# Splitting the load of x by partitions instead of by columns in an 8-expert MLP: staging, semaphores and the last wait

## The chip, the cores and the metric

The kernel runs on one core of a Trainium2 chip. The metric is the device time of one execution in microseconds (us); lower is better. The core has a matrix engine (PE), a vector engine (DVE), a scalar engine (ACT), a general engine (Pool, GpSimd) and a sync engine (SP), each with its own program, and 16 DMA engines that move data between the DRAM (HBM) and the on-chip memory SBUF. SBUF has 128 partitions, and a tensor in it is written [partitions, elements of each partition]. PSUM is the small memory that PE writes its sums to.

## The reference

Eight experts, each with its own weights; no routing, every expert has its 256 rows.

```python
n_experts, capacity, hidden, expert_hidden = 8, 256, 512, 2048
# x [8, 256, 512], w1 [8, 512, 2048], w2 [8, 2048, 512], all float32
h = np.matmul(x, w1)
h = np.maximum(h, 0)
return np.matmul(h, w2).astype(np.float32)
```

The weights are 67.1 MB of float32, x is 4.19 MB and the output 4.19 MB.

## The kernel before

**Layout.** Weights and x are cast to bf16 on the way in. `w1_sb` and `w2_sb` have four slots each (`NS = 4`); expert e uses slot e mod 4. x is first put, rows as they are, into slot 2 of `w2_sb`, under the name `x_sb`: [128, 8192] bf16, where partition p holds 16 rows of x. In DRAM, a partition's 16 rows are 32 KB without a gap. PE transposes it from there into `xT`. `hT` holds the hidden activations of one expert and `out_sb` [128, 8, 2, 512] float32 all outputs. The tensors have fixed places from byte `FIRST_FREE` on; below that, 8 KB were left for the staging tile `x_head`.

**Loading x.** x comes in two parts. The head, the first four of each partition's 16 rows, is loaded by SP as float32 into `x_head` and cast by DVE into `x_sb` (lines 116 and 117). The other twelve rows of each partition are loaded by Pool with the cast done by the DMA (line 131). DMAs issued by Pool are called software_dynamic in the profile, those of SP hardware_dynamic.

**Order of the weights.** All weight loads are issued by Pool, in the order of the list `loads` (lines 99 to 105): w1 and w2 of experts 0 and 1 together, then of 2 and 3, then w1 of 4 and 5, and from there single experts; the last w2 is cut into two halves. A load into a slot that was used before waits until PE has done the expert that used it. The w2 load of experts 2 and 3 overwrites `x_sb`, so it waits for the transposes. Just ahead of the very last weight load stands a tiny store of a few outputs (line 160), which later tells Pool by `d_pool` that the queue has got that far; then Pool stores the outputs of experts 0 to 6 in one transfer (line 172). SP waits for each load in turn and passes it on to PE (`c_w1`, `c_w2`, lines 121 to 123), and at the end stores the outputs of the last expert (line 125).

**Compute.** PE makes the transposes (lines 278 to 304), and then runs a loop over experts: two `half` passes fill `h_ps`, ACT applies the ReLU into `hT` (line 213), and 32 matmuls make `o_ps`, which DVE copies to `out_sb` (line 196); for the last expert ACT copies one half (line 219). The matmul instructions all come from a helper and have line 252, and PE's waits have line 227.

**Semaphores.** PE announces its events on three: `p_xt` (transposes), `p_h` (groups of hidden values) and `p_o` (outputs). `s_ident` counts the two steps that make the identity matrix, `v_out` two points at which DVE has finished outputs. At the very end:

```python
pool.drain()
act.wait_ge(d_pool, 48)
act.wait_ge(d_last, 16).then_inc(s_ident)
```

`d_pool` reaches 48 when the big store has landed, `d_last` 16 when the last one has. After this comes a closing barrier of all engines.

## Time and profile before

| | |
|---|---|
| time, median of 3 | 180.68 us (180.66 to 180.76) |
| span, first to last instruction | 178.9 us |
| PE busy | 129.4 us (72%) |
| ACT, DVE, Pool busy | 38.7, 15.8, 10.3 us |
| moved by DMA | 40.37 MB, mean 226 GB/s |
| Pool's DMA queue, share of 16 engines | 97.2% |
| head of x: size, issue to landing | 1024 KB, 4.9 us |
| rest of x: size written, issue to landing | 1536 KB, 11.6 us |
| weight loads: issue to landing | 43 to 51 us |

The DMA figures count bytes written. A load that turns float32 into bf16 writes half of what it reads, so the same reading rate shows as half the GB/s. "Issue to landing" includes the time that a transfer stands in line behind those issued before it. Where the profile names `w_sb`, it means `w1_sb` or `w2_sb`. "PEq" and "SPq" are the instruction sequencers of those engines.

### The profile page before, as it was taken

How to read it: one execution, taken by the hardware profiler on the slowest of the kernel's cores; microseconds unless marked ns; L12 is line 12 of the kernel's file. 1: busy time of each engine (PE TensorE's matmuls, PEld its weight loads, DVE VectorE, ACT ScalarE, POOL GpSimd, SP SyncE). 2: the span in 40 equal slices, each digit the busy share in tenths (PEclk: the TensorE clock that was granted, in tenths of full speed). 3: DMA queues.
4: the chain of work that ended last, by engine and by line, in shares of the span. 5: the costliest groups of instructions: out<-in, count | busy, mean ns of one | idle time of the engine just before them, and what ended most of it. 6: DMA issues, size and time to landing. Idle time of an engine off the chain costs nothing. (4 is left out here: it accounts for less than half of the span.)

```text
span 178.9 us, 2103 instructions
## 1 busy us (share of the span) xinstructions
PE 129.4 (72%) x832; PEld 90.5 (51%) x832; DVE 15.8 (9%) x20; ACT 38.7 (22%) x38; POOL 10.3 (6%) x21
## 2 busy tenths in 40 slices
PE   0008610793049999995079999999999999969990
PEld 0007610692013696594024884794695696359630
DVE  0204320000000200110000200200200200110010
ACT  0202420053000044044000251152062044004400
POOL 6100010000000002001000100100010000002000
PEclk9999999999756999999859999999999999987997
DMA  6999998999999999899899999999989999999995
GB/s 211 244 216 209 234 227 183 234 231 194 220 234 201 209 234 223 187 234 231 187 227 234 201 209 234 216 194 234 227 187 231 231 194 220 234 189 219 334 423 243
DMA packets 3744, 40.37 MB, mean 226 GB/s; under 512 B 288, under 2 KB 288, under 8 KB 1312
## 3 DMA queue, kind: packets, MB, share of 16 engines
q0 software_dynamic: 3456, 38.80, 97.2%
q1 hardware_dynamic: 288, 1.57, 2.4%
HBM read 71.30 MB, written 4.20 MB: 422 GB/s over the span
## 5 line engine op out<-in xcount | busy, mean ns | idle before, releaser
L252 PE MATMUL o_ps<-w_sb,hT 128*128 x256 | 61.3, 401 | 17.8 <-PEq L227 17.8
L252 PE MATMUL h_ps<-xT,w_sb 128*128 x512 | 62.2, 284 | 11.3 <-PEq L227 11.3
L252 PEld LDWEIGHTS h_ps<-xT,w_sb 128*128 x512 | 58.4, 146 | 15.9 <-issue 13.1
L213 ACT ACTIVATE hT<-h_ps 128x1024 bf16<-128x1024 f32 x32 | 32.7, 1023 | 111.2 <-PE h_ps L252 111.2
L252 PEld LDWEIGHTS o_ps<-w_sb,hT 128*128 128x128 bf16 x256 | 25.6, 102 | 50.7 <-issue 24.5
L196 DVE COPY out_sb<-o_ps 128x512 f32<-128x512 f32 x15 | 9.7, 686 | 141.2 <-PE o_ps L252 141.2
L252 PE MATMUL xt_ps<-identity,w_sb 128*128 128x128 bf16 x64 | 7.6, 311 | 15.6 <-PEq L227 15.6
L252 PEld LDWEIGHTS xt_ps<-identity,w_sb 128*128 x64 | 6.5, 146 | 16.4 <-issue 16.4
L169 POOL DMA_DIRECT2D w_sb<-in_w_dram x12 | 7.4, 619 | 105.1 <-PE h_ps L252 58.0
L179 ACT COPY xT<-xt_ps 128x1024 bf16<-128x1024 bf16 x4 | 4.0, 1012 | 11.7 <-PE xt_ps L252 11.7
L179 DVE COPY xT<-xt_ps 128x1024 bf16<-128x1024 bf16 x4 | 4.9, 1224 | 11.9 <-PE xt_ps L252 11.9
L172 POOL DMA_DIRECT2D out_dram<-out_sb x1 | 1.0, 966 | 33.3 <-DMA out_dram<-out_sb 33.3
L179 ACT ACT_TABLE_LOAD x1 | 1.3, 1283 | 7.2 <-DVE w_sb L117 7.2
L219 ACT COPY out_sb<-o_ps 128x512 f32<-128x512 f32 x1 | 0.6, 585 | 5.9 <-PE o_ps L252 5.9
L117 DVE CAST w_sb<-x_head 128x2048 bf16<-128x2048 f32 x1 | 1.2, 1227 | 5.6 <-DMA x_head<-in_x_dram 5.6
L160 POOL DMA_DIRECT2D out_dram<-out_sb x1 | 0.5, 549 | 14.8 <-DVEq L199 14.8
L131 POOL DMA_DIRECT2D w_sb<-in_x_dram x1 | 0.7, 679 | 0.8 <-POOLq L440 0.8
L135 POOL TENSOR_SCALAR_AFFINE_SELECT identity<-identity 128x128 bf16<-128x128 bf16 x1 | 0.3, 282 | 0.2 <-POOL identity L132 0.2
L132 POOL MEMSET identity<- 128x128 bf16 x1 | 0.2, 223 | 0.0
L440 POOL MEMSET const-float32-0.0<- 128x1 f32 x1 | 0.1, 93 | 0.2 <-issue 0.2
L440 POOL MEMSET const-bfloat16-1.0<- 128x1 bf16 x1 | 0.1, 95 | 0.0
L440 POOL MEMSET const-uint8-127<- 128x1 uint8 x1 | 0.1, 95 | 0.0
(1 smaller groups left out, 0.1 us busy)
## 6 DMA issues: line engine op xcount, KB each, us to landing
w_sb<-in_w_dram POOLq DMA_DIRECT2D x5, 4096.0 KB, 48.0
w_sb<-in_w_dram POOLq DMA_DIRECT2D x5, 2048.0 KB, 51.0
out_dram<-out_sb POOLq DMA_DIRECT2D x1, 3584.0 KB, 12.8
w_sb<-in_w_dram POOLq DMA_DIRECT2D x2, 1024.0 KB, 43.4
w_sb<-in_x_dram POOLq DMA_DIRECT2D x1, 1536.0 KB, 11.6
x_head<-in_x_dram SPq DMA_DIRECT2D x1, 1024.0 KB, 4.9
out_dram<-out_sb SPq DMA_DIRECT2D x1, 512.0 KB, 3.1
out_dram<-out_sb POOLq DMA_DIRECT2D x1, 3.0 KB, 33.8
```

The lines of the kernel that those rows point to most:

```text
L117: nc.vector.tensor_copy(x_sb[:, :HEAD * H], x_head[:])
L131: pool.dma_start(x_sb[:, HEAD * H:], x_v[:, HEAD * H:]).then_inc(d_pool, 16)
L135: pool.affine_select(out=identity[:], in_=identity[:], compare_op=mybir.AluOpType.not_equal, fill=1.0, base=0, pattern=[[-1, P]], channel_ ...
L160: pool.dma_start(out_v[:16, 0:5:2, :16], out_sb[:16, 0:5:2, 0, :16]).then_inc(d_pool, 16)
L169: pool.dma_start(dst, src).then_inc(landed[i][0], 16)
L172: pool.dma_start(out_v[:, :E - 1, :], out_sb[:, :E - 1].rearrange("p e m h -> p e (m h)")).then_inc(d_pool, 16)
L179: return copy(xT[:, ko, m].rearrange("k (ep r2) -> k ep r2", r2=R // MC), xt_ps[m][:].rearrange("k r2 ep -> k ep r2"),)
L196: cp = dve.tensor_copy(out_sb[:, e, m, :], o_ps[m][:])
L213: act.activation(hT[:, g * GJ:(g + 1) * GJ, :].rearrange("p a c -> p (a c)"), h_ps[g % UG][:], mybir.ActivationFunctionType.Relu,).then_in ...
L219: act.copy(out_sb[:, E - 1, 1, :], o_ps[1][:]).then_inc(v_last)
L252: return pe.add_instruction(inst)
L440: nc = _bacc.Bacc("TRN2", target_bir_lowering=False, num_devices=1)
```

## The change

There are three parts.

1. The head of x is cut by partitions. It is now all 16 rows of partitions 0 to 31, 32 KB each, and Pool loads the other 96 partitions whole. The head is still 1 MB, and DVE's cast now covers 32 partitions of 8192 elements. `x_head` takes 32 KB in its partitions. It lies where `out_sb` is, which is moved to the front: the outputs are written only after the head was cast. So the 8 KB kept for the staging tile are given up.
2. PE's three semaphores become one, `s_pe`, whose value is worked out for each event from PE's order of work, and `s_ident` and `v_out` become `s_event`. ACT's wait for the outputs of the expert before is left out, since its next wait on the same counter covers it. One unused semaphore goes.
3. The last waits move from ACT to Pool, and the drain stands between them.

```diff
-FIRST_FREE = 16512 + 8192
+FIRST_FREE = 16512
...
-    HEAD = 4
+    HEAD = 32
...
+    out_sb = allot("out_sb", [P, E, MC, H], FP32)
     w1_sb = allot("w1_sb", [P, NS, K1 * F], BF16)
     w2_sb = allot("w2_sb", [P, NS, K2 * H], BF16)
     xT = allot("xT", [P, K1, MC, E * P], BF16)
     hT = allot("hT", [P, K2, C], BF16)
-    out_sb = allot("out_sb", [P, E, MC, H], FP32)
...
+    s_event = sem("s_event")
+    s_pe, v_last = sem("s_pe"), sem("v_last")
+
+    def after_transposes(n):
+        return s_pe, n
+
+    def after_hidden(e, groups):
+        return s_pe, K1 * MC + e * (NG + MC) + groups
+
+    def after_outputs(e, halves):
+        return s_pe, K1 * MC + e * (NG + MC) + NG + halves
...
-    x_head = x_pool.tile([P, HEAD * H], FP32, tag="x_head")
-    nc.sync.dma_start(x_head[:], x_v[:, :HEAD * H])
-    nc.vector.tensor_copy(x_sb[:, :HEAD * H], x_head[:])
+    x_head = x_pool.tile([HEAD, R * H], FP32, tag="x_head")
+    nc.sync.dma_start(x_head[:], x_v[:HEAD, :])
+    nc.vector.tensor_copy(x_sb[:HEAD, :], x_head[:])
...
-        pool.dma_start(x_sb[:, HEAD * H:], x_v[:, HEAD * H:]).then_inc(d_pool, 16)
+        pool.dma_start(x_sb[HEAD:, :], x_v[HEAD:, :]).then_inc(d_pool, 16)
...
         for e in range(E):
-            if e:
-                act.wait_ge(p_o, MC * e)
             for g in range(NG):
-                act.wait_ge(p_h, e * NG + g + 1)
+                act.wait_ge(*after_hidden(e, g + 1))
...
+        pool.wait_ge(d_pool, 48).then_inc(s_event)
         pool.drain()
-        act.wait_ge(d_pool, 48)
-        act.wait_ge(d_last, 16).then_inc(s_ident)
+        pool.wait_ge(d_last, 16).then_inc(s_event)
```

The other waits on `p_xt`, `p_h`, `p_o`, `s_ident` and `v_out` are rewritten in the same way, each to the count at which the same event has happened.

## The prediction

> **What bounds the kernel now.** I read the page's slices first, then the table of windows, then the DMA queue's own waits, then the chain that ended last, and the timeline at both ends.

> ```profile
> DMA  6999998999999999899899999999989999999995
> q0 software_dynamic: 3456, 38.80, 97.2%
> ```

> The DMA row is full from the second slice to the last but one: 16 DMA engines are the resource that never rests. The table of windows (its last two columns are the mean busy share of the DMA engines and the bytes written) says the same for the stages:

> ```profile
> 0.00:1.74 1.74, 0.00 (x0) 0.00 (x0) 0.00 (x0) 0.00 (x0) 0.70 (x5) 1.00 0.04 5
> 1.74:5.20 3.46, 0.00 (x0) 0.00 (x0) 0.00 (x0) 0.00 (x0) 2.87 (x6) 1.00 1.09 354
> 5.20:12.50 7.30, 0.00 (x0) 0.00 (x0) 1.23 (x1) 1.28 (x1) 0.00 (x0) 1.00 1.06 224
> 12.50:158.20 145.70, 113.55 (x736) 79.57 (x737) 13.91 (x18) 32.69 (x32) 5.76 (x10) 0.94 1.01 216
> ```

> Nothing moves before 1.74; then come the head of x (1.74 to 5.2), the rest of x (5.2 to 12.5) and the weights, each stage at a share of 1. A stage that writes bf16 shows about half the GB/s, because its reads are float32. PE is busy 114 of 146 us in the weight stage: it waits, the DMA engines do not.

> ```profile
> SPq L123 <- DMA w_sb<-in_w_dram: 160.5, 12, 25.3
> SPq L125 <- ACT out_sb L219: 6.8, 1, 6.8
> ```

> SP counts the weight loads off one by one and stands 160.5 of 178.9 us in that wait. Now the end, by the timeline:

> ```profile
> 158.22 8.85 PE L252 MATMUL h_ps<-xT,w_sb 128*128 x64 [2.08 <-PEq L227]
> 166.96 7.07 PE L252 MATMUL o_ps<-w_sb,hT 128*128 x32
> 173.85 0.69 DVE L196 COPY out_sb<-o_ps 128x512 f32<-128x512 f32 x1 [16.60 <-PE o_ps L252]
> 174.06 0.58 ACT L219 COPY out_sb<-o_ps 128x512 f32<-128x512 f32 x1 [5.93 <-PE o_ps L252]
> 174.67 0.35 SPq L125 DMA_DIRECT2D out_dram<-out_sb  x1
> ```

> PE idled 2.08 us before the last expert, until its w1 had landed (the last such packet ends at 157.7). From there 16 us of matmuls, 0.6 us of copy and the last store of 3.1 us lead to 177.8, and 1.1 us of closing to 178.9. The measured 180.68 is 1.8 more than this span. So whatever moves the landing of the last w1 moves the end one for one, and since its queue never runs dry, that landing is the sum of all DMA work ahead of it, the loading of x included. The big output store (last packets near 176.15) is behind the same stream and shifts alike.

> The start, where the change is:

> ```profile
> 0.74 0.38 SPq L116 DMA_DIRECT2D x_head<-in_x_dram  x1
> 1.24 0.68 POOL L131 DMA_DIRECT2D w_sb<-in_x_dram  x1 [0.79 <-POOLq L440]
> 2.81 2.19 POOL L169 DMA_DIRECT2D w_sb<-in_w_dram  x3 [0.16 <-issue]
> 5.62 1.23 DVE L117 CAST w_sb<-x_head 128x2048 bf16<-128x2048 f32 x1 [5.62 <-DMA x_head<-in_x_dram]
> 7.18 1.28 ACT L179 ACT_TABLE_LOAD   x1 [7.18 <-DVE w_sb L117]
> 13.37 1.63 PEld L252 LDWEIGHTS xt_ps<-identity,w_sb 128*128 x16 [13.37 <-issue]
> ```

> The trace's packet records give the stages per DMA engine: the head is 8 packets of 8192 B on each of 16 engines, first starts 1.97 on the mean, most packets 309 ns, the first two or so 0.5 to 1.1 us. The rest of x is 8 packets (24 KB read, 12 KB written) of 926 ns, mean first start 4.91; the weights are packets of 32 KB read, 16 KB written, every 1.210 us, mean first start 12.22. On each engine the rest of x begins some 10 ns after that engine's own head is done, though it was issued at 1.24: the second transfer queues behind the first.

> [...] The trace has only 128-partition loads; its head, 1.05 MB from 1.74 to 5.21, makes 302 GB/s[...].

> **The change part by part.**

> *The head.* The same 1.05 MB, as 32 packets of 32 KB, two per engine, all into partitions 0 to 31. [...] 8 x 0.309 = 2.47 before[...]. Before, the head occupied an engine 4.91 - 1.97 = 2.94 us, so 0.47 was start-up. [...] I take 2.25[...].

> *The rest of x.* 96 rows, 6 packets per engine of the weights' size: 6 x 1.210 = 7.26 against 12.22 - 4.91 = 7.31: -0.05. Its writes are half its reads, 13.5 GB/s per engine[...].

> *The cast on DVE.* 32 partitions of 8192 elements in place of 128 of 2048. The time goes with the length of a row: 4 x 1.227 = 4.9 us at most, 4.4 if about 0.16 of the 1.227 is fixed. Start 5.62 + 2.25 = 7.9, end 12.8 at the latest. Behind it stand the entry branches of SP, ACT and DVE and ACT's table load (1.28). They are hidden by the rest of x, which lands at about 12.5 + 2.2 = 14.7; PE waits for that, then for the first weights until 32.4 + 2.2. [...] Cost 0.

> *Staging in out_sb.* Its first output copy is at 61.3 us, long after the cast. Cost 0; 8 KB of SBUF freed.

> *One counter for PE's events.* PE does its work in program order, so a count of all events passes at the instruction at which the three counters did. The number of increments is the same. ACT loses seven waits (17 ns each by the row of L212), all under the weight stream. Pool's three load waits keep their place: its loads are issued tens of us ahead of the DMA engines (w1 of experts 4 and 5 at 68.95, in line behind loads that last to about 90). Cost 0.

> *Pool waits last.* Before, Pool's drain began at 163.71 and lasted 13.49, to 177.20, while ACT's wait for the last store ended at 177.78. Now Pool waits for the big store, drains, and waits for the last store. The drain should end near 177.2, 0.5 before that store lands, so the end is still set by it, with one hop from Pool in place of one from ACT: 0, within 0.1 either way. Nobody else stands behind Pool's waits but the closing barrier, which needed the last store anyway.

> *Sum.* +2.25 - 0.05 + 0 = +2.2 on the DMA stream, carried one for one to the end: 180.68 + 2.2 = 182.9.

> **Rivals.** (a) [...] the DMA engines, not SBUF, set the pace as before, and the head takes 2.4 us plus start-up. For it: an engine alone makes 26.5 GB/s[...]. Time 180.7, or down to 180.2 if fewer, longer packets save the start-up of 0.47. That lower part ends on the other side: faster. (b) [...] the rest of x fills the gaps[...]. Both loads read 4.19 MB, at 16 x 26.7 GB/s (32 KB in 1.227 us) 9.8 us[...], so the whole could hide, giving 180.6 to 181.2. Against: the strict order seen on every engine. (c) [...] Pool's drain now lasts past the last landing (a drain of the old tail, 177.20 - 176.5 = 0.7, put after it): 183.3 to 183.8.

> **How the numbers follow.** [...] 1.9 to 2.4 us more: 0.68. (c) 0.09. (a) 0.13, about half of it faster by more than 0.2% (0.36 us) and half level. (b) 0.10, one part in three each faster, level and slower. So faster 0.10, same 0.10, slower 0.80. The range runs from 180.6, which takes in most of (b) and the upper part of (a), to 183.4[...].

> **What would show it.** Right: head packets of about 2.4 us, the issue-to-landing time of the head from 4.9 to about 7.1, the first packets of the rest of x near 7.1, first transposes near 15.6, the last expert's first matmul near 160.4, and the stretch from there to the end unchanged at 20.7. The forecast is wrong if the head's packets take 1.2 us (a), or if they take 2.4 but those of the rest of x start among them and the weights still start at 12.2 (b). If the head grows but the last w1 does not land later, the one-for-one step is wrong.

## The result, and the profile after

The kernel after takes 182.88 us (182.79 to 182.92) against 180.72 for the kernel before, measured beside it: a ratio of 1.0119, 95% interval 1.0101 to 1.0136. It is 2.2 us (1.2%) slower, as forecast (182.9).

The start of the kernel after, from its timeline (start, duration, engine, line, what):

```profile
0.74 0.39 SPq L129 DMA_DIRECT2D x_head<-in_x_dram  x1
1.25 0.65 POOL L144 DMA_DIRECT2D w_sb<-in_x_dram  x1 [0.80 <-POOLq L451]
8.33 4.42 DVE L130 CAST w_sb<-x_head 32x8192 bf16<-32x8192 f32 x1 [8.33 <-DMA x_head<-in_x_dram]
13.07 1.28 ACT L192 ACT_TABLE_LOAD   x1 [13.07 <-DVE w_sb L130]
15.47 1.63 PEld L263 LDWEIGHTS xt_ps<-identity,w_sb 128*128 x16 [15.47 <-issue]
```

Both loads of x are issued when they were, but DVE gets the head at 8.33 us where it got it at 5.62, and its cast ends at 12.75, where before it was done at 6.85. That delay is hidden: PE starts its transposes only when the rest of x is there, at 15.47, 2.1 later than before. The page's list of DMA issues (KB each, us from issue to landing) puts the growth at the loads themselves:

```profile
w_sb<-in_x_dram POOLq DMA_DIRECT2D x1, 1536.0 KB, 13.7
x_head<-in_x_dram SPq DMA_DIRECT2D x1, 1024.0 KB, 7.6
```

The head went from 4.9 to 7.6, the rest of x from 11.6 to 13.7. The table of windows, cut at the new stage ends (last columns: mean share of the DMA engines, GB/s written):

```profile
1.74:7.50 5.76, 0.00 (x0) 0.00 (x0) 0.00 (x0) 0.00 (x0) 2.86 (x6) 1.00 1.06 233
7.50:14.70 7.20, 0.00 (x0) 0.00 (x0) 4.42 (x1) 1.28 (x1) 0.00 (x0) 1.00 1.00 214
14.70:160.40 145.70, 110.89 (x730) 78.91 (x738) 13.92 (x18) 32.72 (x32) 5.77 (x10) 0.94 1.01 216
```

In the first stage the engines count as busy all the time (a share of 1.06), as they did before (1.09), but write 233 GB/s instead of 354: the busy share doesn't tell the two paces apart. A window of the weight stage that is as long as before, but cut 2.2 us later, shows the same 216 GB/s. The end, by the timeline:

```profile
160.31 8.96 PE L263 MATMUL h_ps<-xT,w_sb 128*128 x64 [2.64 <-PEq L238]
169.16 7.07 PE L263 MATMUL o_ps<-w_sb,hT 128*128 x31
176.88 0.36 SPq L138 DMA_DIRECT2D out_dram<-out_sb  x1
```

The trace's packet records show the two heads side by side. "First" and "latest" are over the first packet of each of the 16 engines, in us.

```text
                                         before          after
head packets per engine, bytes           8 x 8192        2 x 32768
one head packet, median ns               309             2544
rest of x, mean first / latest           4.91 / 5.22     6.82 / 7.34
weights, mean first / latest             12.22 / 12.52   14.18 / 14.65
last 16 KB weight packet ends            157.71          159.83
big store's last packet ends             176.15          178.28
last store's last packet ends            177.40          179.53
```

The records do not name the engine of a packet; a first packet is taken as one of the 16 earliest of its load. The shift arises before the rest of x starts: 1.91 us on the mean engine, 2.12 on the latest. At the last weight packet and the two stores it is 2.12, 2.13 and 2.13 us, so the latest engine's shift is the one that the kernel pays.

### The profile page after: what moved, and what is told of

The parts are those of the page before. It is cut to its first block, busy times and chain, and to the rows that moved or that the text cites. A ratio compares the mean times of both kernels' runs of the same rounds, so it can differ in the third digit from the quotient of the medians.

```text
span 181.1 us, 2089 instructions
## 1 busy us (share of the span) xinstructions
PE 126.7 (70%) x824; PEld 89.7 (50%) x832; DVE 19.0 (11%) x20; ACT 38.7 (21%) x38; POOL 10.3 (6%) x21
## 3 DMA queue, kind: packets, MB, share of 16 engines
q0 software_dynamic: 3424, 38.80, 96.0%
## 5 line engine op out<-in xcount | busy, mean ns | idle before, releaser
L263 PE MATMUL o_ps<-w_sb,hT 128*128 x248 | 59.2, 393 | 20.0 <-PEq L238 19.3
L263 PE MATMUL h_ps<-xT,w_sb 128*128 x512 | 61.4, 282 | 11.8 <-PEq L238 11.8
L263 PEld LDWEIGHTS h_ps<-xT,w_sb 128*128 x512 | 57.9, 146 | 16.2 <-issue 12.5
L224 ACT ACTIVATE hT<-h_ps 128x1024 bf16<-128x1024 f32 x32 | 32.8, 1024 | 111.2 <-PE h_ps L263 111.2
L263 PEld LDWEIGHTS o_ps<-w_sb,hT 128*128 128x128 bf16 x256 | 25.3, 101 | 51.3 <-issue 24.6
L130 DVE CAST w_sb<-x_head 32x8192 bf16<-32x8192 f32 x1 | 4.4, 4415 | 8.3 <-DMA x_head<-in_x_dram 8.3
L173 POOL DMA_DIRECT2D out_dram<-out_sb x1 | 0.5, 549 | 14.7 <-DVEq L212 14.7
## 6 DMA issues: line engine op xcount, KB each, us to landing
w_sb<-in_x_dram POOLq DMA_DIRECT2D x1, 1536.0 KB, 13.7
```

Of the source, the lines that this page charges most:

```text
L130: nc.vector.tensor_copy(x_sb[:HEAD, :], x_head[:])
L173: pool.dma_start(out_v[:16, 0:5:2, :16], out_sb[:16, 0:5:2, 0, :16]).then_inc(d_pool, 16)
L224: act.activation(hT[:, g * GJ:(g + 1) * GJ, :].rearrange("p a c -> p (a c)"), h_ps[g % UG][:], mybir.ActivationFunctionType.Relu,).then_in ...
L263: return pe.add_instruction(inst)
```

## The experiments

The theory: the head is slow because of the partitions that it writes, 0 to 31. In the kernel after, an engine writes a packet of 32 KB in about 2.55 us; 16 engines at that pace make 205 GB/s, an estimate from the packet records, where 8 KB in 309 ns makes 424 in the kernel before. The rivals: long packets or few partitions are slow in themselves; the merged counters or Pool's waits cost something; the queues' order was chance.

**Each half of the change alone.** First the kernel after with the old head:

```diff
-    HEAD = 32
+    HEAD = 4
...
-    x_head = x_pool.tile([HEAD, R * H], FP32, tag="x_head")
-    nc.sync.dma_start(x_head[:], x_v[:HEAD, :])
-    nc.vector.tensor_copy(x_sb[:HEAD, :], x_head[:])
+    x_head = x_pool.tile([P, HEAD * H], FP32, tag="x_head")
+    nc.sync.dma_start(x_head[:], x_v[:, :HEAD * H])
+    nc.vector.tensor_copy(x_sb[:, :HEAD * H], x_head[:])
...
-        pool.dma_start(x_sb[HEAD:, :], x_v[HEAD:, :]).then_inc(d_pool, 16)
+        pool.dma_start(x_sb[:, HEAD * H:], x_v[:, HEAD * H:]).then_inc(d_pool, 16)
```

> The kernel after, with x's head cut by columns again (128 partitions of 8 KB); one counter, staging in out_sb and Pool's last waits stay. Theory [...]: head packets back at about 0.31 us, weights start near 12.2 us, time 180.7 within 0.3. Rival (part of the loss is the waits on Pool or the merged counters): head packets at 0.31 us, but the time stays 0.5 or more above 180.7.

It took 180.79 us, 1.0007 of the kernel before (0.9998 to 1.0016), with head packets of 309 ns and weights from 12.30. With the head by columns the loss is gone.

Then the kernel before with the new head, and `out_sb` moved under it:

```diff
-FIRST_FREE = 16512 + 8192
+FIRST_FREE = 16512
...
-    HEAD = 4
+    HEAD = 32
...
-    x_head = x_pool.tile([P, HEAD * H], FP32, tag="x_head")
-    nc.sync.dma_start(x_head[:], x_v[:, :HEAD * H])
-    nc.vector.tensor_copy(x_sb[:, :HEAD * H], x_head[:])
+    x_head = x_pool.tile([HEAD, R * H], FP32, tag="x_head")
+    nc.sync.dma_start(x_head[:], x_v[:HEAD, :])
+    nc.vector.tensor_copy(x_sb[:HEAD, :], x_head[:])
...
```

The move of `out_sb` to the front and Pool's load of the other partitions, left out here, are as in the change itself.

> The kernel before, with only the head cut by partitions and staged in out_sb; its three counters and ACT's last waits stay. Theory: head packets of 1.8 to 2.7 us, time 182.8 within 0.3, as the kernel after. Rival (waits and counters carry part): between 181.0 and 182.3.

It took 182.73 us, 1.0114 of the kernel before (1.0097 to 1.0131), with a median head packet of 2556 ns. The head carries nearly the whole loss.

These two runs showed something else. Here is the end of the first, by its timeline:

```profile
158.20 7.31 PE L263 MATMUL h_ps<-xT,w_sb 128*128 x64 [1.61 <-PEq L238]
171.66 0.81 PE L263 MATMUL o_ps<-w_sb,hT 128*128 x3
172.51 0.58 ACT L230 COPY out_sb<-o_ps 128x512 f32<-128x512 f32 x1 [5.93 <-PE o_ps L263]
173.12 0.35 SPq L138 DMA_DIRECT2D out_dram<-out_sb  x1
```

PE was done 1.6 us earlier than in the kernel before (its first pass over the last expert took 7.31 us in place of 8.85), and SP issued the last store at 173.12 instead of 174.67. Yet that store's last packet ended at 177.47, against 177.40. Its first packet started at 175.76, 2.6 us after the issue, where in the kernel before it was 0.96 us (174.67 to 175.63). In both that is some 0.5 us ahead of the end of the big store's last packet (176.22 here, 176.15 before), however early the last store was issued: its packets stand in line behind the big store's. In the second run SP issued at 175.25, 1.6 earlier than the kernel after, and the last packet ended at 179.51 against 179.53. So here the end is set by the DMA engines all the way, not by PE's last expert.

**Which partitions.** Two kernels load as the head 1 MB of 64 partitions, half a row each. They differ in the partitions alone: 0 to 63, or 32 to 95. The theory takes the first for slow, like the head on partitions 0 to 31, and the second for as fast as the head by columns; this was the author's estimate, shown by no trace until then. Pool loads the rest in three pieces in both, and the waits that count Pool's loads of x are raised by two loads in both.

```diff
-    x_head = x_pool.tile([HEAD, R * H], FP32, tag="x_head")
-    nc.sync.dma_start(x_head[:], x_v[:HEAD, :])
-    nc.vector.tensor_copy(x_sb[:HEAD, :], x_head[:])
+    x_head = x_pool.tile([P, HALF], FP32, tag="x_head")
+    nc.sync.dma_start(x_head[HEAD:HEAD + 64, :], x_v[HEAD:HEAD + 64, :HALF])
+    for p in (HEAD, HEAD + 32):
+        nc.vector.tensor_copy(x_sb[p:p + 32, :HALF], x_head[p:p + 32, :])
...
-        pool.dma_start(x_sb[HEAD:, :], x_v[HEAD:, :]).then_inc(d_pool, 16)
+        pool.dma_start(
+            x_sb[HEAD:HEAD + 64, HALF:], x_v[HEAD:HEAD + 64, HALF:]
+        ).then_inc(d_pool, 16)
+        for p in (64, 96):
+            pool.dma_start(x_sb[p:p + 32, :], x_v[p:p + 32, :]).then_inc(d_pool, 16)
...
```

That is the form with `HEAD = 0`; the other has `HEAD = 32` and the pieces at 0 and 96.

> The head is half a row (16 KB) of partitions 0 to 63: again 1 MB, half as long a packet, twice as many partitions[...]. Pool loads the rest in three transfers. Theory [...]: 1.05 MB at the 205 GB/s that the kernel after shows [...] is 5.1 us, packets of about 1.28 us, first weights near 14.3, time 182.8 to 183.2. Rival (32 KB packets of SP's queue are slow in themselves, or 32 partitions are too few): packets of about 0.61 us, first weights near 12.3, time 180.7 to 181.0.

> As the run with partitions 0 to 63, but the half rows are those of partitions 32 to 95[...]. Theory [...]: packets of about 0.61 us, first weights near 12.3, time 180.7 to 181.0, about 2 us under its twin. Rival (number of partitions or packet length decides): the same time as its twin.

The list of DMA issues, partitions 0 to 63:

```profile
x_head<-in_x_dram SPq DMA_DIRECT2D x1, 1024.0 KB, 7.9
```

and partitions 32 to 95:

```profile
x_head<-in_x_dram SPq DMA_DIRECT2D x1, 1024.0 KB, 5.2
```

The packets have a median of 1275 and 611 ns, as expected, and the times are 183.41 and 181.40 us: 1.0151 (1.0134 to 1.0168) and 1.0042 (1.0025 to 1.0059). The same bytes, packet length, partition count and instructions, and a source in DRAM that is moved by 1 MB but otherwise alike, 2.0 us apart: neither packet length nor the number of partitions makes this difference, but which partitions. What it is about them is not shown. Both came out above their forecasts, by 0.2 and 0.4 us. The head's first packet starts 0.3 to 0.4 later than in the kernel after (2.08 and 2.13 against 1.77), and SP's issue takes 0.54 and 0.60 us against 0.39; why stays open. Part is at the other end: Pool's drain takes 1.45 us in both, against 1.29 in the kernel after, and the stretch from the last packet to the end of the span 1.83 and 1.76 us against 1.59.

**Half and double the head.** Only `HEAD` changes, to 16 and to 64 whole partitions.

```diff
-    HEAD = 32
+    HEAD = 16
```

> The kernel after with a head of 16 whole partitions: half the bytes, one 32 KB packet per engine[...]. Theory [...] as long as the head of 32; the rest grows to 7 packets of 1.21 us. First weights near 15.8, time about 184.5, 1.6 above the kernel after although less is loaded slowly. Rival (each long packet costs 2.5 us): one packet in place of two, 1.3 less in the head, 1.2 more in the rest: about 182.8.

```diff
-    HEAD = 32
+    HEAD = 64
```

> The kernel after with a head of 64 whole partitions: twice the bytes [...]. Theory: 2.1 MB at 205 GB/s is 10.2 us, four packets of 2.55 per engine; the rest is 64 partitions [...], 4 packets that write 13.5 GB/s per engine[...]. First weights near 17.5, time about 186.2. Rival (the growth is a start-up cost of the first packets): first weights near 14.2, time about 182.9. If the cast on DVE (4.4 us, ending near 17) comes to matter, first transposes move but not the time.

With 16 partitions:

```profile
x_head<-in_x_dram SPq DMA_DIRECT2D x1, 512.0 KB, 8.1
```

Half the bytes land later than the 1024 KB of the kernel after (7.6). A fixed price per long packet would have had them land earlier. But the time was 183.09 us, 1.0134 (1.0118 to 1.0149), far under the 184.5 of the theory and nearer to the rival's 182.8. The packet records tell why. A head packet is recorded as 3.0 to 4.1 us (2.5 by the rival), and the engine then goes on to its first packet of the rest of x, which takes 1.4 to 2.1 us in place of 1.23. Some of the writes to the head's semaphore meanwhile take up to 3.3 us, until 8.20 (12 to 20 ns in the kernel after). So the end of the landing runs beside the first packets of the rest of x, and part of it is hidden: the stream was delayed by 2.4 us, where the landing came 3.2 later than before. What holds these writes up is not shown.

With 64 partitions the time was 185.54 us, 1.0268 (1.0252 to 1.0283), 2.7 above the kernel after; 186.2 was expected. The head's packets have a median of 2546 ns, so the price grows with the bytes and is no start-up; but each engine's first and fourth take 2.21 and 2.28 us on the mean, which makes four of them 0.6 us shorter than the forecast had it. The cast ended at 20.2 and the transposes began at 20.98, with no effect on the weight stream. One surprise: the records show 48 head packets, then 16 of the rest of x (from 9.06 us on), and then the last 16 head packets, each starting as one of those 16 ends. By that, every engine took one packet of the rest ahead of its fourth head packet: the order of the two queues is not strict here. The 2.12 of the kernel after is here 4.84 us, at the latest engine's first weights (17.36 against 12.52) and again at the last store's last packet (182.24 against 177.40).

**No head.** SP's load and DVE's cast are dropped, Pool loads all of x.

```diff
-    x_head = x_pool.tile([HEAD, R * H], FP32, tag="x_head")
-    nc.sync.dma_start(x_head[:], x_v[:HEAD, :])
-    nc.vector.tensor_copy(x_sb[:HEAD, :], x_head[:])
...
-        pool.dma_start(x_sb[HEAD:, :], x_v[HEAD:, :]).then_inc(d_pool, 16)
+        pool.dma_start(x_sb, x_v).then_inc(d_pool, 16)
```

> The kernel after without a head: Pool loads all of x with the cast in the DMA, and DVE's cast goes. Shows when Pool's first packet is ready if nothing stands before it. Theory (in both kernels the rest of x stood in line behind the head): first packet between 2.5 and 3.7 us, then 8 packets of 1.21, first weights 12.3 to 13.5, time 180.7 to 182.0, faster than the kernel after. Rival (Pool's packets are ready only at about 4.6, and the order seen was chance): first weights near 14.3, time near 182.9.

The first packet of Pool's load starts at 2.61 us, the weights at 13.29 on the mean, and the time is 181.79 us, 1.0064 (1.0048 to 1.0079). As Pool issues its load at the same time in all three, the rest of x was ready 2 us and more before it ran in both kernels (4.69 us at the earliest before, 6.11 after), and stood behind the head. And the head by partitions is worse than none: by columns it saves 1.1 us over no head, by partitions it loses 1.1.

**The last waits.** The head by columns, with the drain moved ahead:

```diff
-        pool.wait_ge(d_pool, 48).then_inc(s_event)
         pool.drain()
+        pool.wait_ge(d_pool, 48).then_inc(s_event)
         pool.wait_ge(d_last, 16).then_inc(s_event)
```

> As the run with the head cut by columns, but Pool drains before its two last waits instead of between them. Theory: in the kernel after the drain ended 0.5 us past the last store's last packet and after it Pool's wait; with the drain first the wait ends when the store lands, some 0.38 after its last packet as in the kernel before, so the closing is 0.1 to 0.2 shorter than with the drain between: about 180.6. Rival (the drain costs the same wherever it is): no difference in the time from the last packet to the end.

It took 180.66 us, 0.9998 of the kernel before (0.9990 to 1.0007). The drain, in the kernel after (first line) and here (second), as the trace lists it (duration in ns, start in us):

```profile
L435 POOLq DRAIN  x1: 1288/1288/1288, 178.7 to 178.7; - x1
```

```profile
L434 POOLq DRAIN  x1: 13499/13499/13499, 164.1 to 164.1; - x1
```

Between the waits the drain starts when the big store has landed and costs 1.29 us, to 180.02. Started early, it is over 1.03 us after the big store's last packet (177.59 and 176.55). The drain between the waits holds back Pool's last wait, which passes at 180.07, 0.54 after the last store's last packet; drained ahead, it passes 0.37 after it, as ACT's did before (0.38). So 0.17 us of closing belongs to the drain's place. In the measured times the two forms (1.0007 and 0.9998 of the kernel before) have intervals that overlap, so this rests on the traces.

## Why the prediction was right

- **The bound.** From the latest engine's first weight packet to the last weight packet it takes 145.19 us before and 145.18 after, and the shift came through one for one. Right, but one step of the chain was put down to the wrong thing. The text led the end through PE's last expert and mentioned the big store as behind the same stream; the runs show that the two were close and that the store is the one that counts. Nothing in the forecast hung on it, since both move with the stream.
- **The head.** The size was right: packets of about 2.4 us were forecast, and they took 2.54 on the median, 1.8 to 2.7 in all. But the forecast of a slow head, its 2.4 and its 2.25 us were the author's estimates, which no trace of the kernel before showed; the runs show that the partitions slow the packets down, but not how. The sum of 2.25 agrees with the 2.12 of the latest engine partly by luck. The prediction counted from an engine's first head packet to its first packet of the rest of x, on the mean, and put the growth of that at 2.25. By this measure the growth is 1.65 here, under the low end of the forecast 1.9 to 2.4, and 2.00 in the run with the head alone. The other 0.47 here comes from two things that it left out: the head's first packets start 0.26 us later (2.23 on the mean against 1.97), and the latest engine counts, not the mean one (0.21). Its signs were off in opposite directions: the first packets of the rest of x came at 6.82 on the mean (about 7.1 forecast), the landing of the head took 7.6 us (7.1).
- **Landing and engines.** The landing grew by 2.7 us, the stream by 2.1. The head's last packet is recorded to end at 7.35 us, and DVE gets it at 8.33, 0.98 later; before, it was 0.41 (5.21 and 5.62). The pair on 64 partitions has the same split, 1.10 us with partitions 0 to 63 and 0.39 with 32 to 95. So some 0.6 us of the slow landing don't hold up the engines.
- **Which partitions.** The pair of runs on 64 partitions bears out that they decide: a head packet of 16 KB took 1275 ns with 0 to 63 and 611 with 32 to 95. In the kernel after the head's 32 packets ran in two rounds of 16, two per engine as forecast: the first 16 are all under way from 2.78 to 3.56 us, where the second round begins.
- **The rest of x.** Forecast -0.05; mean first weight less mean first packet gives 7.36 us against 7.31, so +0.05.
- **The cast.** 4.42 us, the low one of the two bounds (4.4 with a fixed part of 0.16), hidden as said. The two casts, 1.227 us for 2048 elements and 4.415 for 8192, give a fixed part of 0.16 too, an estimate that takes the rest as even. It took the same 4.42 with 16 and with 64 partitions: the length of a row sets its time, as the prediction had it.
- **Counters and staging.** Nothing clear of noise, as the first experiment shows.
- **Pool's last waits.** Forecast 0 within 0.1, with the drain ending near 177.2 before the shift, that is 179.3. It ended at 180.02, since it takes 1.29 us once the store has landed. The small sum is luck in part: the drain adds 0.16 to 0.17, and the hop from Pool instead of ACT gives back 0.08 (from the last wait to the end of the span 1.06 us, 1.13 before). Net +0.08, as the spans show (1.59 from the last packet to the end, 1.51 before).
- **Rivals.** (a), the DMA engines at their pace as before, fell with the packets of 2.54 us. (b), the rest of x filling the gaps, was mostly wrong for this head, yet something of the kind exists: the hidden 0.6 us, more of it with 16 partitions, and the fourth packet's turn with 64. The engines' first packets of the rest of x were stretched to 1.4 to 2.1 us with 16 partitions, took 1.26 to 1.36 with 32 and 1.23 to 1.27 with 64, where the median weight packet of the kernel after took 1.227; why is not shown. (c) is off in size, but its drain after the wait was real.

The sum as measured in the traces: 2.12 in the stream, 0.08 in the closing, 2.2 in all.

## What to carry to other kernels

When the DMA engines are the bound, time lost at the first load is paid at the end, whatever slack the compute engines have: here 2.12 us at the start were 2.13 at the end, and 4.84 were 4.84. Mind which partitions a load writes: whole rows of partitions 0 to 31 made fewer and longer packets, 32 of 32 KB in place of 128 of 8 KB, but one took 2.54 us on the median, where the same bytes took 4 x 0.309 = 1.24 spread over 128 partitions, and the engines still showed as busy. 1 MB to 64 partitions cost 2.0 us less where they were 32 to 95 than where they were 0 to 63. Look at the bytes per second of the stage and at the duration of one packet, not at the busy share. And put a drain of Pool ahead of the last waits for stores, not between them: that saved 0.17 us in the traces, too little to show in the times.
